# First norm of a hybrid decoder step: scale the rows of x before the transposes, and transpose raw x in a place of its own

## The chip, the cores and the metric

One core of a Trainium2 chip runs the whole kernel as one launch. The metric is the device time of one execution in microseconds (us), median of several runs. TensorE is called PE in the profile, VectorE DVE, ScalarE ACT, GpSimd POOL, and SyncE, whose queue starts the DMAs, SP.

## The reference, cut to what matters

One layer of a decoder trunk is computed for 512 prompt positions and for 8 samples of 8 positions, 576 tokens in all, with 1024 features. The part that matters here is the first norm and what uses x:

```python
def rmsnorm(x, w):
    xf = xf * lax.rsqrt(jnp.mean(xf * xf, axis=-1, keepdims=True) + EPS)
    return (xf * w.astype(F32)).astype(x.dtype)
...
    xn = rmsnorm(x, norm1_w)
    proj = xn @ w_in            # 1024 x 6928, feeds four token mixers
    gates = sigmoid(xn @ w_merge + b_merge)
    x = x + merged @ w_out      # raw x comes back here
    x = x + ConvFFN(rmsnorm(x, norm2_w))
```

(The last five lines are condensed from the reference.) So the token factor rsqrt(mean(x^2)) belongs to a row of x, the weight norm1_w to a column, and the raw x is wanted again only much later, for the residual sum.

## The kernel before, in words

All big products are done on PE in three passes (high x high, high x low, low x high), so each operand is split into a rounded part `hi` and a remainder `lo`. The activations stand transposed: `K.xh[k]` and `K.xl[k]`, k = 0..7, hold 128 features by 576 tokens each (columns 0 to 511 prompt, 512 to 575 samples).

`front` makes them. It loads x in five tiles `xt` (tokens on partitions; four of 128 prompt tokens, one of 64 sample tokens), sums the squares per token (`ss`: ACT for tiles 0, 2, 4, DVE for 1 and 3), takes Sqrt on ACT and a reciprocal on DVE, and turns the factors on PE into a tile `rb` in which every partition holds the factors of all 576 tokens. Apart from that, PE transposes raw x (32 transposes of 128x128 for the prompt, 8 of 64x128 for the samples); ACT copies the result to `xT0..7` and `xTs`. DVE multiplies `xT` by norm1_w and `rb` into `xn` (line 387), ACT rounds `xn` to `xh`, and DVE (for k = 2 and 5 POOL) subtracts for `xl` (line 170, in `split`). The sample columns go the same way in one tile `xns` on POOL. All of that has the highest priority, 3 * HIGH.

`front` returns `vectors`, which `dense_stream` calls after the first projection, "u". Before the change it finishes the loads of small vectors (three transposes into the banks `dn`, copied by DVE at line 140) and stores `xTt` and `xTs` to DRAM (lines 396 and 397); the tail reads them for the residual.

`dense_stream` is the long chain of products: "u" (4 panels of w_in, each 2 column halves x 24 matmuls of 128x288), then "rw", "hg" and so on. Each half uses one PSUM bank of the pool `dn`, which has two banks; ACT evacuates it. Two streams of mixers run beside it with priority HIGH. The raw weights are loaded three panels ahead (`wraw`, 3 buffers) and split by ACT (`whi`) and DVE or POOL (`wlo`).

The program order on each engine is laid out when the kernel is built: a scheduler takes instructions by priority along a simulated timeline, and gives out buffers of a pool as they come free there. On the chip each engine then runs its list strictly in that order. So an edit at one place can lay later instructions out in another order too.

Of the kernel before, what the change touches and what calls it, by code (L numbers as in the profile page):

```python
# [8 lines left out]
F32 = mybir.dt.float32  # L9
F32R = mybir.dt.float32r  # L10
AF = mybir.ActivationFunctionType
ALU = mybir.AluOpType
# [3 lines left out]
P = 128  # L16
D = 1024
TP = 512
NS = 8
LS = 8  # L20
T = TP + NS * LS
# [3 lines left out]
EPS = 1e-6  # L25
# [15 lines left out]
class Kern:  # L41
# [49 lines left out]
    def turn(self, out, x):  # L91

        sl = slice(x.base_partition(), x.base_partition() + x.shape[0])
        self.nc.tensor.transpose(out, x, self.ident[sl, sl])  # L94
# [230 lines left out]
def front(K):  # L325

    nc, tc, I = K.nc, K.tc, K.I
    K.columns()
    K.xh = [K.xnp.tile([P, T], F32R, name=f"xh{k}") for k in range(8)]
    K.xl = [K.xnp.tile([P, T], F32R, name=f"xl{k}") for k in range(8)]  # L330
    xTd = K.dram.tile([8, P, T], F32, name="xTd")
    K.xT = [xTd[k] for k in range(8)]
    xp, xs = I["x_prompt"][0], I["x_sample"].rearrange("b t d -> (b t) d")
    fp = K.fp
    with tc.high_priority(offset=3 * HIGH):
        pre = fp.tile([P, 1], F32, name="pre")
        nc.scalar.activation(pre, K.eps, AF.Sqrt)
        xt = []
        for i in range(5):
            r = P if i < 4 else T - 4 * P  # L340
            t = fp.tile([P, D], F32, name=f"xt{i}")
            nc.sync.dma_start(out=t[:r, :], in_=xp[i * P:(i + 1) * P, :] if i < 4 else xs)
            xt.append((t, r))
            if i == 0:
                K.load_group(0, fp)()

        ss = fp.tile([P, 5], F32, name="ssq")
        nc.vector.memset(ss, 1.0)
        for i, (t, r) in enumerate(xt):
            q = fp.tile([P, D], F32, tag=f"xq{i % 2}", bufs=1, name=K.n("xq"))  # L350
            if i % 2:
                nc.vector.tensor_tensor(out=q, in0=t, in1=t, op=ALU.mult)
                nc.vector.tensor_reduce(out=ss[:, i:i + 1], in_=q, op=ALU.add, axis=mybir.AxisListType.X)
            else:
                nc.scalar.activation(q[:r, :], t[:r, :], AF.Square, accum_out=ss[:r, i:i + 1])
        nc.scalar.activation(ss, ss, AF.Sqrt, bias=K.eps, scale=1.0 / D)
        nc.vector.reciprocal(out=ss, in_=ss)
        rb = fp.tile([P, T], F32, name="rb")
        pb = K.ps(of="b")
        for i, (t, r) in enumerate(xt):  # L360
            if i == 4:
                nc.vector.tensor_copy(out=rb[:, :TP], in_=pb)
                pb = K.ps(of="b")
            o = i * P if i < 4 else 0
            K.turn(pb[:, o:o + r], ss[:r, i:i + 1].to_broadcast([r, P]))
        nc.vector.tensor_copy(out=rb[:, TP:], in_=pb[:, :T - TP])

        t, r = xt[4]
        ps = K.ps(of="b")
        for k in range(8):  # L370
            K.turn(ps[:, k * r:(k + 1) * r], t[:r, k * P:(k + 1) * P])
        pv = ps.rearrange("p (k t) -> p k t", k=8)
        xTs = fp.tile([P, 8, r], F32, name="xTs")
        nc.scalar.copy(out=xTs, in_=pv)
        xns = fp.tile([P, 8, r], F32, name="xns")
        nc.gpsimd.tensor_tensor(out=xns, in0=xTs, in1=K.vcs("norm1_w", 0, 8).unsqueeze(2).to_broadcast([P, 8, r]), op=ALU.mult)
        nc.gpsimd.tensor_tensor(out=xns, in0=xns, in1=rb[:, TP:].unsqueeze(1).to_broadcast([P, 8, r]), op=ALU.mult)
        xTt = []
        for k in range(8):
            ps = K.ps(of=("a", "a0", "a2", "a0")[k % 4])  # L380
            for i in range(4):
                K.turn(ps[:, i * P:(i + 1) * P], xt[i][0][:, k * P:(k + 1) * P])
            xT = fp.tile([P, TP], F32, name=f"xT{k}")
            nc.scalar.copy(out=xT, in_=ps)
            xTt.append(xT)
            xn = fp.tile([P, TP], F32, tag="xn", bufs=3, name=K.n("xn"))
            nc.vector.scalar_tensor_tensor(out=xn, in0=xT, scalar=K.vc("norm1_w", k), in1=rb[:, :TP], op0=ALU.mult, op1=ALU.mult)
            K.split(K.xh[k][:, :TP], K.xl[k][:, :TP], xn, nc.gpsimd if k in (2, 5) else nc.vector)
            K.split(K.xh[k][:, TP:], K.xl[k][:, TP:], xns[:, k], nc.gpsimd)
    rest = [K.load_group(i, fp) for i in range(1, len(K.vgroups))]  # L390

    def vectors():
        for turn in rest:
            turn()
        for k in range(8):
            nc.sync.dma_start(out=K.xT[k][:, :TP], in_=xTt[k])
        nc.sync.dma_start(out=xTd[:, :, TP:].rearrange("k p t -> p k t"), in_=xTs)
        K.halve("rw_w0", "rw_a0", "b_merge", "ssd_conv_b", "s5_glu_b", "ssd_conv_w")
    return vectors

# [1906 lines left out]
@with_exitstack  # L2307
def hybrid_step(ctx, tc, I, O):
    K = Kern(ctx, tc, I, O)
    e = ctx.enter_context  # L2310
    K.xnp = e(tc.tile_pool(name="xn", bufs=1))
    K.stage = e(tc.tile_pool(name="stage", bufs=2))
    K.wraw = e(tc.tile_pool(name="wraw", bufs=3))
    K.wsp = e(tc.tile_pool(name="wsp", bufs=5))
    K.fc = ExitStack()
    K.fp = K.fc.enter_context(tc.tile_pool(name="front", bufs=1))
    K.vectors = front(K)
    drive(K, [(mix_stream(K, "a", ("rw",)), "a"), (mix_stream(K, "b", ("s5", "hg", "ssd")), "b"), (dense_stream(K), None)])
    K.spare = {"t": ["c"]}
    K.banks(4, c=2, w=2)  # L2320
    K.stream = "t"
    tail(K)
    K.pst.close()
# [26 lines left out]
```

## Time and profile before

| what | value |
|---|---|
| median of 3 runs | 1688.13 us |
| lowest, highest run | 1680.99, 1700.95 us |
| the profiled execution, its own time | 1685.1 us |
| its span, first to last instruction | 1683.4 us |
| PE busy | 1591.3 us (95%) |
| DVE, ACT, POOL busy | 70%, 41%, 47% |
| mean granted PE clock | 0.965 of full |

The busy shares are means over the whole span; the first 65 us, where the change lies, look different from the rest. The lowest and the highest run of the same kernel stand 1.2% apart.

### The profile page before, as it was taken

How to read it: one execution, taken by the hardware profiler on the slowest of the kernel's cores; microseconds unless marked ns; L12 is line 12 of the kernel's file. 1: busy time of each engine (PE TensorE's matmuls, PEld its weight loads, DVE VectorE, ACT ScalarE, POOL GpSimd, SP SyncE). 2: the span in 40 equal slices, each digit the busy share in tenths (PEclk: the TensorE clock that was granted, in tenths of full speed). 3: DMA queues.
4: the chain of work that ended last, by engine and by line, in shares of the span. 5: the costliest groups of instructions: out<-in, count | busy, mean ns of one | idle time of the engine just before them, and what ended most of it. 6: DMA issues, size and time to landing. Idle time of an engine off the chain costs nothing. (4 is left out here: it accounts for less than half of the span.)

```text
span 1683.4 us, 33091 instructions
## 1 busy us (share of the span) xinstructions
PE 1591.3 (95%) x12344; PEld 1445.8 (86%) x12344; DVE 1179.6 (70%) x2566; ACT 691.8 (41%) x1489; POOL 785.4 (47%) x1013
## 2 busy tenths in 40 slices
PE   5998999999999999999999999998999999999997
PEld 4987888888788888878888888998998999899997
DVE  7888886988684398343367553685489966975985
ACT  6333232333433345233244443432456634643653
POOL 5545342444522454232354542375667734744750
PEclk7999897899999999899999999999999999999999
DMA  7545452544472365343265543764323232232232
GB/s 202 136 122 152 130 140 59 159 136 113 134 202 73 101 165 173 87 104 93 87 178 148 169 133 106 233 199 142 112 84 89 80 109 63 88 89 82 82 108 72
DMA packets 356453, 207.64 MB, mean 123 GB/s; under 512 B 110884, under 2 KB 328357, under 8 KB 356293
## 3 DMA queue, kind: packets, MB, share of 16 engines
q1 hardware_dynamic: 356293, 205.53, 43.6%
q8 instruction: 97, 1.59, 0.4%
q14 instruction: 63, 0.52, 0.1%
HBM read 151.54 MB, written 53.02 MB: 122 GB/s over the span
## 5 line engine op out<-in xcount | busy, mean ns | idle before, releaser
L224 PE MATMUL dn<-xl,whi 128*128 128x288 f32 x1392 | 425.6, 306 | 2.0 <-DVE xl L170 1.6
L223 PE MATMUL dn<-xh,whi 128*128 128x288 f32 x1392 | 424.9, 306 | 2.4 <-ACT gst L432 0.9
L225 PE MATMUL dn<-xh,wlo 128*128 128x288 f32 x1392 | 424.9, 305 | 0.0
L225 PEld LDWEIGHTS dn<-xh,wlo 128*128 128x128 f32 x1392 | 267.6, 192 | 14.6 <-issue 11.2
L223 PEld LDWEIGHTS dn<-xh,whi 128*128 128x128 f32 x1392 | 267.5, 192 | 14.3 <-issue 7.3
L224 PEld LDWEIGHTS dn<-xl,whi 128*128 128x128 f32 x1392 | 267.6, 192 | 12.8 <-issue 6.2
L169 ACT CAST whi<-wraw 128x512 fp32r<-128x512 f32 (+1 forms) x278 | 173.5, 628 | 234.8 <-PE dn L224 227.3
L170 POOL TENSOR_TENSOR wlo<-wraw,whi 128x512 fp32r<-128x512 f32 x92 | 127.4, 1385 | 170.6 <-ACT whi L169 162.7
L170 DVE TENSOR_TENSOR wlo<-wraw,whi 128x512 fp32r<-128x512 f32 (+1 forms) x186 | 156.1, 841 | 66.4 <-ACT whi L169 58.0
L262 PE MATMUL dn<-big,whi 128*128 128x288 f32 x528 | 108.6, 298 | 8.7 <-DVE raw L679 2.9
L247 POOL TENSOR_TENSOR wlo<-wraw,whi 128x512 fp32r<-128x512 f32 x66 | 90.1, 1372 | 48.1 <-ACT whi L246 48.0
L262 PE MATMUL dn<-xh,whi 128*128 128x288 f32 x352 | 104.8, 299 | 4.7 <-ACT whi L246 4.0
L223 PE MATMUL dn<-yh,whi 128*128 128x288 f32 x352 | 103.9, 299 | 4.5 <-DVE g L489 3.3
L262 PE MATMUL dn<-xh,wlo 128*128 128x288 f32 x352 | 103.6, 298 | 4.4 <-POOL wlo L247 4.4
L224 PE MATMUL dn<-yl,whi 128*128 128x288 f32 x352 | 104.6, 298 | 2.1 <-DVE yl L167 2.1
L225 PE MATMUL dn<-yh,wlo 128*128 128x288 f32 x352 | 104.7, 299 | 0.0
L262 PE MATMUL dn<-xl,whi 128*128 128x288 f32 x352 | 103.5, 295 | 0.0
L223 PE MATMUL dn<-ah,whi 128*128 128x288 f32 (+2 forms) x324 | 95.1, 298 | 1.5 <-ACT ah L169 1.5
L224 PE MATMUL dn<-al,whi 128*128 128x288 f32 (+2 forms) x324 | 95.5, 296 | 0.6 <-DVE al L170 0.6
L262 PEld LDWEIGHTS dn<-big,whi 128*128 128x128 f32 x528 | 84.3, 188 | 12.4 <-ACT su L286 4.5
L225 PE MATMUL dn<-ah,wlo 128*128 128x288 f32 (+2 forms) x324 | 95.0, 295 | 0.0
L262 PE MATMUL dn<-big,wlo 128*128 128x288 f32 x264 | 77.7, 295 | 0.1
(749 smaller groups left out, 4105.6 us busy)
## 6 DMA issues: line engine op xcount, KB each, us to landing
wraw<-w_in SPq DMA_DIRECT2D x55, 512.0 KB
wraw<-ffn_up SPq DMA_DIRECT2D x44, 512.0 KB
wraw<-w_merge SPq DMA_DIRECT2D x32, 512.0 KB
gate<-gst SPq DMA_DIRECT2D x32, 288.0 KB
g<-gate SPq DMA_DIRECT2D x32, 288.0 KB
wraw<-ffn_down SPq DMA_DIRECT2D x16, 448.0 KB
pd_hg<-st SPq DMA_DIRECT2D x16, 288.0 KB
wraw<-w_br_ssd SPq DMA_DIRECT2D x8, 512.0 KB
```

The costliest lines, as they stand in the source:

```text
L169: nc.scalar.copy(out=hi, in_=src)
L170: lo_engine.tensor_tensor(out=lo, in0=src, in1=hi.bitcast(F32), op=ALU.subtract)
L223: nc.tensor.matmul(ps, wh, xh[k][:, sl], start=k == 0, stop=False)
L224: nc.tensor.matmul(ps, wh, xl[k][:, sl], start=False, stop=False)
L225: nc.tensor.matmul(ps, wl, xh[k][:, sl], start=False, stop=k == len(wt) - 1)
L247: TT[eng](out=lo, in0=src, in1=hi.bitcast(F32), op=ALU.subtract)
L262: nc.tensor.matmul(ps, wt[:, k], x, start=start and k == 0 and i == 0, stop=k == n - 1 and i == 2, skip_group_check=not start)
```

## The change

The sum of squares of tile 3 moves from DVE to ACT, and the factor is computed by DVE alone, with eight small operations on a 128x5 tile (`K.rsqrt`: one bit trick and two Newton steps), so the Sqrt on ACT and its early table load go. There is no `rb` any more: each row tile of x is multiplied by its factors into `xr` (tiles 0 and 2 on ACT, 1 and 3 on DVE, 4 on POOL). PE transposes `xr`. The split then reads the PSUM bank directly, with norm1_w as its scale: ACT writes `xh` and DVE `xl` for all eight k. The sample columns follow after the eight prompt groups. Raw x is transposed a second time inside `vectors`, after "u": for each k four prompt transposes into one bank `dn`, one sample transpose into another, two copies by ACT into a tile `xT` (2 buffers), and one store of 288 KB.

```diff
--- before.py
+++ after.py
@@ -333,8 +333,6 @@
     xp, xs = I["x_prompt"][0], I["x_sample"].rearrange("b t d -> (b t) d")
     fp = K.fp
     with tc.high_priority(offset=3 * HIGH):
-        pre = fp.tile([P, 1], F32, name="pre")
-        nc.scalar.activation(pre, K.eps, AF.Sqrt)
         xt = []
         for i in range(5):
             r = P if i < 4 else T - 4 * P
@@ -346,55 +344,54 @@
 
         ss = fp.tile([P, 5], F32, name="ssq")
         nc.vector.memset(ss, 1.0)
+        xr = [fp.tile([P, D], F32, name=f"xr{i}") for i in range(5)]
         for i, (t, r) in enumerate(xt):
-            q = fp.tile([P, D], F32, tag=f"xq{i % 2}", bufs=1, name=K.n("xq"))
-            if i % 2:
-                nc.vector.tensor_tensor(out=q, in0=t, in1=t, op=ALU.mult)
-                nc.vector.tensor_reduce(out=ss[:, i:i + 1], in_=q, op=ALU.add, axis=mybir.AxisListType.X)
+            if i == 1:
+                nc.vector.tensor_tensor(out=xr[i], in0=t, in1=t, op=ALU.mult)
+                nc.vector.tensor_reduce(out=ss[:, i:i + 1], in_=xr[i], op=ALU.add, axis=mybir.AxisListType.X)
             else:
-                nc.scalar.activation(q[:r, :], t[:r, :], AF.Square, accum_out=ss[:r, i:i + 1])
-        nc.scalar.activation(ss, ss, AF.Sqrt, bias=K.eps, scale=1.0 / D)
-        nc.vector.reciprocal(out=ss, in_=ss)
-        rb = fp.tile([P, T], F32, name="rb")
-        pb = K.ps(of="b")
+                nc.scalar.activation(xr[i][:r, :], t[:r, :], AF.Square, accum_out=ss[:r, i:i + 1])
+        nc.vector.tensor_scalar(out=ss, in0=ss, scalar1=1.0 / D, scalar2=EPS, op0=ALU.mult, op1=ALU.add)
+        rs, y1, y2 = (fp.tile([P, 5], F32, name=f"rsq{i}") for i in range(3))
+        K.rsqrt(rs, ss, y1, y2)
+
         for i, (t, r) in enumerate(xt):
-            if i == 4:
-                nc.vector.tensor_copy(out=rb[:, :TP], in_=pb)
-                pb = K.ps(of="b")
-            o = i * P if i < 4 else 0
-            K.turn(pb[:, o:o + r], ss[:r, i:i + 1].to_broadcast([r, P]))
-        nc.vector.tensor_copy(out=rb[:, TP:], in_=pb[:, :T - TP])
-
-        t, r = xt[4]
-        ps = K.ps(of="b")
-        for k in range(8):
-            K.turn(ps[:, k * r:(k + 1) * r], t[:r, k * P:(k + 1) * P])
-        pv = ps.rearrange("p (k t) -> p k t", k=8)
-        xTs = fp.tile([P, 8, r], F32, name="xTs")
-        nc.scalar.copy(out=xTs, in_=pv)
-        xns = fp.tile([P, 8, r], F32, name="xns")
-        nc.gpsimd.tensor_tensor(out=xns, in0=xTs, in1=K.vcs("norm1_w", 0, 8).unsqueeze(2).to_broadcast([P, 8, r]), op=ALU.mult)
-        nc.gpsimd.tensor_tensor(out=xns, in0=xns, in1=rb[:, TP:].unsqueeze(1).to_broadcast([P, 8, r]), op=ALU.mult)
-        xTt = []
+            f = rs[:r, i:i + 1]
+            if i in (0, 2):
+                nc.scalar.activation(xr[i][:r, :], t[:r, :], AF.Copy, scale=f)
+            else:
+                (nc.gpsimd if i == 4 else nc.vector).tensor_scalar(out=xr[i][:r, :], in0=t[:r, :], scalar1=f, scalar2=None, op0=ALU.mult)
         for k in range(8):
             ps = K.ps(of=("a", "a0", "a2", "a0")[k % 4])
             for i in range(4):
-                K.turn(ps[:, i * P:(i + 1) * P], xt[i][0][:, k * P:(k + 1) * P])
-            xT = fp.tile([P, TP], F32, name=f"xT{k}")
-            nc.scalar.copy(out=xT, in_=ps)
-            xTt.append(xT)
-            xn = fp.tile([P, TP], F32, tag="xn", bufs=3, name=K.n("xn"))
-            nc.vector.scalar_tensor_tensor(out=xn, in0=xT, scalar=K.vc("norm1_w", k), in1=rb[:, :TP], op0=ALU.mult, op1=ALU.mult)
-            K.split(K.xh[k][:, :TP], K.xl[k][:, :TP], xn, nc.gpsimd if k in (2, 5) else nc.vector)
+                K.turn(ps[:, i * P:(i + 1) * P], xr[i][:, k * P:(k + 1) * P])
+            K.split(K.xh[k][:, :TP], K.xl[k][:, :TP], ps, None, K.vc("norm1_w", k))
+
+        r = T - TP
+        ps = K.ps(of="b")
+        for k in range(8):
+            K.turn(ps[:, k * r:(k + 1) * r], xr[4][:r, k * P:(k + 1) * P])
+        xns = fp.tile([P, 8, r], F32, name="xns")
+        nc.vector.tensor_tensor(out=xns, in0=ps.rearrange("p (k t) -> p k t", k=8),
+                                in1=K.vcs("norm1_w", 0, 8).unsqueeze(2).to_broadcast([P, 8, r]), op=ALU.mult)
+        for k in range(8):
             K.split(K.xh[k][:, TP:], K.xl[k][:, TP:], xns[:, k], nc.gpsimd)
     rest = [K.load_group(i, fp) for i in range(1, len(K.vgroups))]
 
     def vectors():
         for turn in rest:
             turn()
+
         for k in range(8):
-            nc.sync.dma_start(out=K.xT[k][:, :TP], in_=xTt[k])
-        nc.sync.dma_start(out=xTd[:, :, TP:].rearrange("k p t -> p k t"), in_=xTs)
+            xT = fp.tile([P, T], F32, tag="xT", bufs=2, name=K.n("xT"))
+            for lo, hi in ((0, 4), (4, 5)):
+                ps = K.psdense()
+                n = (hi - lo) * P if lo == 0 else T - TP
+                for i in range(lo, hi):
+                    t, r = xt[i]
+                    K.turn(ps[:, (i - lo) * P:(i - lo) * P + r], t[:r, k * P:(k + 1) * P])
+                nc.scalar.copy(out=xT[:, lo * P:lo * P + n], in_=ps[:, :n])
+            nc.sync.dma_start(out=K.xT[k], in_=xT)
         K.halve("rw_w0", "rw_a0", "b_merge", "ssd_conv_b", "s5_glu_b", "ssd_conv_w")
     return vectors
 
```

`K.rsqrt`, `K.split`, `K.turn` and `K.psdense` are unchanged. `split` with a scale is the form that the second half of the kernel used already:

```python
        if scale is not None:
            nc.scalar.activation(hi, src, AF.Copy, scale=scale)
            nc.vector.scalar_tensor_tensor(out=lo, in0=src, scalar=scale, in1=hi.bitcast(F32), op0=ALU.mult, op1=ALU.subtract)
            return
```

## Rows read from the trace of the kernel before

**Rows 1.** The page, parts 1 and 2: busy time, and the clock in 40 slices.

```profile
PE 1591.3 (95%) x12344; PEld 1445.8 (86%) x12344; DVE 1179.6 (70%) x2566; ACT 691.8 (41%) x1489; POOL 785.4 (47%) x1013
...
PEclk7999897899999999899999999999999999999999
```

**Rows 2.** Windows: each engine's busy time, then PE clock, DMA share, GB/s.

```profile
24.00:37.00 13.00, 8.32 (x29) 6.21 (x29) 13.00 (x23) 7.49 (x27) 10.01 (x10) 0.50 0.69 217
37.00:61.00 24.00, 23.69 (x177) 23.23 (x176) 22.21 (x108) 11.12 (x22) 9.71 (x23) 1.00 0.64 161
61.00:64.40 3.40, 0.70 (x6) 0.24 (x4) 3.26 (x15) 0.92 (x2) 2.69 (x8) 0.99 0.40 66
200.00:1250.00 1050.00, 1018.52 (x8180) 899.04 (x8180) 666.38 (x1405) 388.42 (x862) 457.56 (x552) 0.96 0.47 134
```

**Rows 3.** Timeline, 12 to 24 us: start, length, engine, line, operation.

```profile
14.53 0.19 ACT L355 ACTIVATION_READ_ACCUMULATOR xq<-xt 64x1 f32 x1
...
15.56 2.06 ACT L169 CAST whi<-wraw 128x512 fp32r<-128x512 f32 x2
...
17.93 0.32 ACT L356 ACTIVATE ssq<-ssq,epsc 128x5 f32<-128x5 f32 x1
...
18.96 0.85 PE L94 MATMUL mx<-ident,ssq 128*128 128x128 f32 x5 [2.02 <-DVE ssq L357]
...
22.21 3.14 DVE L387 SCALAR_TENSOR_TENSOR xn<-xT,vecs,rb 128x512 f32<-128x512 f32 x3
...
23.81 0.61 PE L223 MATMUL dn<-xh,whi 128*128 128x288 f32 x1 [0.46 <-ACT xh L169]
```

**Rows 4.** Timelines of DVE and POOL, 37 to 40 us: the last pieces of xl.

```profile
37.67 0.68 DVE L170 TENSOR_TENSOR xl<-xn,xh 128x512 fp32r<-128x512 f32 x1
...
37.68 1.98 POOL L170 TENSOR_TENSOR xl<-xns,xh 128x64 fp32r<-128x64 f32 x5
```

**Rows 5.** Groups by line and shape, 0 to 45 us: count, busy us, mean ns.

```profile
L387 DVE SCALAR_TENSOR_TENSOR xn<-xT,vecs,rb 128x512 f32<-128x512 f32 x8 | 6.9, 889 | 0.0
...
L170 DVE TENSOR_TENSOR xl<-xn,xh 128x512 fp32r<-128x512 f32 x6 | 5.0, 834 | 0.0
...
L384 ACT COPY xT<-mx 128x512 f32<-128x512 f32 x8 | 4.5, 602 | 1.4 <-PE mx L94 1.4
...
L1048 DVE TENSOR_SCALAR exk<-exk 128x16 f32<-128x16 f32 x4 | 0.7, 168 | 0.1
```

**Rows 6.** Line 94, transposes of x, 12 to 13 us and 16.5 to 17 us: ns min/median/max.

```profile
L94 PE MATMUL mx<-ident,xt x4: 421/421/476, 12.1 to 12.8; 128*128 128x128 f32 x4
L94 PEld LDWEIGHTS mx<-ident,xt x4: 183/228/231, 12.1 to 12.6; 128*128 128x128 f32 x4
...
L94 PE MATMUL mx<-ident,xt x4: 273/314/421, 16.1 to 16.7; 128*128 128x128 f32 x4
L94 PEld LDWEIGHTS mx<-ident,xt x2: 140/178/217, 16.4 to 16.6; 128*128 128x128 f32 x2
```

**Rows 7.** Timeline, 61 to 70 us: the end of "u" and the vectors stage.

```profile
61.01 0.27 PE L94 MATMUL dn<-ident,vraw 128*128 128x128 f32 x1
...
63.33 0.40 PE L94 MATMUL dn<-ident,vraw 128*128 128x128 f32 x2 [2.05 <-DVE vecs L140]
...
64.38 0.61 PE L223 MATMUL dn<-xh,whi 128*128 128x288 f32 x1 [0.66 <-DVE vecs L140]
...
69.40 0.40 ACT L414 COPY st<-dn 128x288 f32<-128x288 f32 x1 [7.41 <-DMA wup<-rw_a_up]
```

**Rows 8.** Timeline of SP's queue, 73 to 83 us: stores and reloads of a 288 KB panel.

```profile
73.81 0.53 SPq L422 DMA_DIRECT2D pd_rw<-st  x1
79.43 0.33 SPq L1465 DMA_DIRECT2D raw<-pd_rw  x1
79.88 0.36 SPq L422 DMA_DIRECT2D pd_rw<-st  x1
...
82.50 0.46 SPq L1465 DMA_DIRECT2D raw<-pd_rw  x1
```

**Rows 9.** PE's waits, 90 to 200 us: total us, times, longest.

```profile
PE mxrw L1571 <- DVE tB L1565: 5.3, 2, 4.7
```

**Rows 10.** Line 1165, a DVE copy of 256 elements: ns min/median/max.

```profile
L1165 DVE COPY s5br<-s5u x1: 281/281/281, 57.2 to 57.2; 128x256 f32<-128x256 f32 x1
```

## The prediction, as it was put on record

> **What bounds the kernel now.** I read the page first, then windows by stage, then the timeline of the first 70 us, then waits. PE is busy for 95% of the span [rows 1], and between 200 and 1250 us it works 1018.5 of 1050 us while no other engine passes 64% [rows 2]: from there on the kernel is PE's own pace, and a microsecond that the dense products lose or win early is still there at the end. The change lies ahead of that, in two places with other limits. From 24 to 37 us DVE is busy for all of 13.0 us, and PE, at half clock, makes only 29 instructions where it makes 177 in the next 24 us [rows 2]: there the products wait for the pieces of xh and xl. From 61.0 to 64.4 us, after "u", PE works 0.7 us of 3.4 [rows 2]: it waits 2.05 and 0.66 us for DVE to empty the banks of the small vectors, while ACT stands idle for 7.41 us [rows 7].
>
> At 37 to 61 us a product takes 24/177 = 0.136 us. "u" has 192 of them, 26 us; it ends at 61.0, so it ends as if it had run at full pace from 35.0. What the front wins is how far that point moves forward.
>
> **The front, part by part.** *Head.* The last sum of squares is there at 14.72, but Sqrt runs on ACT only at 17.93, behind two rounding casts of weights (15.56, 2.06 us); then come the reciprocal, PE's turn at 18.96, the copies to `rb`, and the first `xn` at 22.21; the first product starts at 23.81 [rows 3]. After: eight dependent DVE operations on 128x5. A DVE operation on 128x16 takes 0.168 us [rows 5], so 1.3 us, taken as 1.6 with the handovers (an estimate): factors at 16.3. The casts still fill ACT until 17.6. Then `xr` 0 and 2 on ACT: twice the elements of an `xT` copy (0.602 us [rows 5]), so 1.2 us each at most, until 20.0. `xr` 1 and 3 on DVE: four times the copy of 256 elements in 0.281 us [rows 10], 1.1 us each at most, done before. `xr` 4 on POOL is needed last. The last transpose of the first group and ACT's `xh` (0.6 us) give 20.9 for the first product: 2.9 us earlier.
>
> *Body.* From 22.21 to the last prompt `xl`, 38.35 [rows 3, 4], are 16.1 us of DVE: 6.9 for eight `xn`, 5.0 for six `xl` [rows 5], so 4.2 for other work (weight splits, the S5 tables). After, the eight `xn` are gone, but all eight `xl` are DVE's, in the two-operand form that line 387 has now, and from PSUM. The nearest rows are 0.834 and 0.889 us [rows 5]; with 0.85 that is 6.8, plus one `xns` of 0.85 and the same 4.2: 11.9 us from 20.9, so 32.8, 5.6 us earlier. ACT loses eight `xT` copies (4.5 us) and gains two `xr` (2.4) and one square; its eight `xh` stay. PE now has the transposes on the path: 0.23 us apart at half clock [rows 6], 0.92 for a group of four, about the same pace as DVE's 0.85. *Sample columns.* POOL takes 1.98/5 = 0.40 us for each of eight small `xl`, 3.2 us, and ends at 39.66 now [rows 4]; after, with `xns` made near 31.5, at about 35, 4.7 us earlier, and the products of the second half are wanted only then. POOL also loses two large `xl` and two multiplications.
>
> I take 5.5 us for the front, between the two. Its bounds: 2.9, if only the head is won, and 8, if some 2.5 us of DVE's other work slips behind the front.
>
> The stores of xT leave SP's queue near 31 us. I cost that at nothing: the weights of "u" were split by then or are loaded three panels ahead. Without this cover it would be a gain. The early Sqrt and its table load ran before x had landed: nothing too.
>
> **Raw x, the price.** Eight groups now stand between "u" and "rw". For a group PE fills one bank `dn` with four transposes, ACT empties it, and the next group wants that bank again, because the other holds the sample columns. So PE and ACT take turns. The transposes: 3 x 0.14 + 0.27 = 0.7 us at full clock, 3 x 0.23 + 0.42 = 1.1 at half [rows 6]; the copy 0.6 [rows 5]; two handovers of 0.1 (an estimate). That is 1.5 to 1.9 us for a group, 12.0 to 15.4 for eight; PE's busy share of some half leaves the clock open, so I take 1.75, 14 us. ACT has the room (7.41 us idle, eight copies of 0.6 and eight of the sample's, smaller). Behind the waiting transposes stand on PE the first products of "rw", which want the same two banks; behind the copies on ACT the next weight casts; on SP, behind stores that wait for ACT, the loads for RWKV and the next panel of w_in. The panels for "rw" already landed cover that.
>
> What hides some of it: the 2.7 us in which PE waits for DVE at this very place [rows 7]. Two banks serve both, so I count 1 us (0 to 2.7). Later, between 90 and 200 us, PE waits 5.3 us in a mixer for DVE [rows 9]; if the mixer's DVE work is not late as well, part of the delay ends there. But that mixer is fed by "rw", which is late; I count 1.5 (0 to 5.3).
>
> The clock, first as the rows show it: transposes of 421 ns at 12.1 to 12.8 us become 273 ns at 16.7, when PE had run nothing but transposes for four microseconds [rows 6]; so here a stretch of transposes alone brought the full clock. The Trainium skill (TensorE: Matmul & The Clock Gate, Part 4: PE-mode transpose) says that transposes do not engage the full clock; the trace disagrees. By that rule all groups would run at half clock, 15.4 us in place of 14, and the front's groups at 0.92 in place of 0.85, 0.6 later. It would make the change 2.0 us worse, the fourth case below.
>
> **Sum.** -5.5 + 14 - 1 - 1.5 = +6.0 us. The profiled execution, 1685.1, becomes 1691; it stands 3.0 under the median of the runs, 1688.13, which becomes 1694. A difference under 1% (17 us) is about what a measurement of this kernel can't tell from no change: its three runs lie 1.2% apart.
>
> **Rivals.** *Hidden.* All terms at their good ends: -8 + 12 - 2.7 - 5.3 = -4, 1684. For it: ACT and DVE's waits leave room just there; against it: one bank per group is a strict turn, and PE is the pace later. *Stores, the slow side.* `xT` has two buffers, so the copy of group k+2 waits until the store of k has landed. Two stores of the same size show bounds: issued 79.88, read back from 82.50 on, at most 2.6 us; issued 73.81, read back at 79.43, at most 5.6 [rows 8]. With a copy and a sample copy of 0.8, a group takes half of (landing + 0.8): 1.7 us at 2.6, hidden beneath the banks; 3.2 at 5.6, 25.6 us for eight: -5.5 + 25.6 - 2.5 = +17.6, 1706. From a landing of about 2.7 us on it sets the pace; from 5.4 on the loss passes 1%. *It doesn't speed the front.* If DVE, with all `xl` from PSUM, keeps the pace of now, only the head's 2.9 is left: -2.9 + 14 - 2.5 = +8.6, 1697. *Clock rule.* By the case above +8.0, 1696; the row speaks against it. *Laid out anew.* Everything behind is ordered by a simulated timeline, so stages far from the change can shift. The mean clock of 0.965 means 3.5% of 1683 us, 59 us, lost to half clock, in slices all along [rows 1]; a quarter of that either way is 15 us: 1679 or 1709 around the forecast. Nothing in the profile says which way.
>
> **Chances.** Forecast, with its terms between the ends, 0.40; hidden 0.20; stores 0.12; front not faster 0.08; clock rule 0.04; anew, better 0.08, worse 0.08. The range of 8 in 10 goes from 1677 to 1708: it leaves out about half of each outer case and the spread of a median of such runs. Faster by over 1% (under 1671): 0.07, the better half of "anew" and the tail of "hidden". Slower by over 1% (over 1705): 0.16, most of "stores" and "anew, worse". The rest, 0.77, lies within.
>
> **What the profile after would show.** If the steps are right: no `xn` group, eight `xl` of some 0.85 us on DVE from PSUM, the first product near 21 us, "u" ending near 55.5 in place of 61.0; then eight groups at `dn`, transposes of xt alternating with ACT copies, 1.5 to 1.9 us each, and the first product of "rw" near 71 in place of 64.4. Stores as the limit would show as ACT's copies waiting for a DMA. What would make it wrong: raw transposes that run inside "u" or between products, in gaps that cost nothing; groups paced by stores; a front that still waits, for the clock or for casts on ACT ahead of `xr`; or PE's half-clock stretches after 100 us moving by more than both terms.

## The result, and the profile after

| kernel | median us | lowest to highest | runs | ratio to before, 95% interval |
|---|---|---|---|---|
| before | 1683.94 | 1677.81 to 1700.95 | 22 | |
| after | 1697.47 | 1689.5 to 1712.43 | 22 | 1.0083 (1.0063 to 1.0103) |

The change makes the kernel 0.8% slower: 13.5 us by the medians, 11 to 17 by the interval. The median lies 3.5 us over the forecast of 1694, inside the range of 1677 to 1708 and inside "within 1%". In part that is luck. The difference was forecast as +6 and came out twice as large; and the three runs of before that the forecast stood on had a median of 1688.13, where these 22 have 1683.94, from which the sum gives 1690. So the sum has to be gone through. The profiled execution of after took 1691.0 us (span 1689.3), the very figure of the sum; that is luck too, for it is the third lowest of its 22 runs, while that of before stood 1.2 us over the median of its kernel. A single pair of traces differs here by 5.9 us where the medians differ by 13.5.

The page of after, parts 1 and 2, against [rows 1]:

```profile
PE 1589.9 (94%) x12379; PEld 1446.4 (86%) x12379; DVE 1163.9 (69%) x2566; ACT 699.2 (41%) x1498; POOL 784.9 (46%) x1010
...
PEclk9788887999999999999999999999999999999999
```

PE is still the bound; span less busy time, it was idle for 99.4 us in place of 92.1. In the clock line the first slice of 42 us rose from 0.7 to 0.9 of the full clock, the second fell from 0.9 to 0.7: the new front won clock, and the raw-x stage lost it. But the line flatters the start. The profile records no clock ahead of the first rise, at 16.5 us in before and 25.4 in after, and the line counts that time as full; the transposes below show that it was half. The windows of the same stretches, against [rows 2] (busy time of PE, PEld, DVE, ACT, POOL, then PE clock, DMA share, GB/s):

```profile
24.00:37.00 13.00, 12.99 (x99) 12.22 (x98) 11.63 (x35) 9.22 (x27) 5.23 (x13) 1.00 0.49 134
...
54.20:77.80 23.60, 18.57 (x102) 13.94 (x100) 21.15 (x83) 8.39 (x22) 7.19 (x19) 0.64 0.43 121
...
20.00:24.00 4.00, 3.68 (x17) 3.45 (x17) 3.84 (x5) 3.56 (x6) 4.00 (x3) 1.00 0.47 97
...
59.50:76.60 17.10, 16.22 (x87) 12.64 (x88) 15.05 (x52) 5.97 (x17) 2.96 (x5) 0.50 0.40 126
```

From 24 to 37 us PE makes 99 instructions, from 25.4 on at full clock; it made 29 at half. "u" ends at 54.2 in place of 60.9, and what stood between it and the first product of "rw" has grown from 3.4 us to 23.6, at 0.64 of the clock: PE is at half from 59.5 to 76.6.

The head of the front, timeline of after, against [rows 3]:

```profile
13.44 0.17 DVE L354 TENSOR_SCALAR ssq<-ssq 128x5 f32<-128x5 f32 x1 [4.54 <-ACT xr L353]
...
14.46 0.21 DVE L1082 COPY s5ldb<-s5ld 16x128 f32<-16x128 f32 x1 [0.85 <-DMA s5ld<-s_log_dt]
14.61 0.15 DVE L176 TENSOR_SCALAR rsq<-ssq 128x5 int32<-128x5 int32 x1
...
15.07 1.08 DVE L170 TENSOR_TENSOR wlo<-wraw,whi 128x512 fp32r<-128x512 f32 x1
...
16.14 1.08 DVE L170 TENSOR_TENSOR wlo<-wraw,whi 128x512 fp32r<-128x512 f32 x1
16.84 1.77 POOL L170 TENSOR_TENSOR wlo<-wraw,whi 128x512 fp32r<-128x512 f32 x1 [13.80 <-ACT whi L169]
17.13 1.49 DVE L178 TENSOR_TENSOR rsq<-rsq 128x5 f32<-128x5 f32 x1
...
18.86 0.17 DVE L180 SCALAR_TENSOR_TENSOR rsq<-rsq,rsq 128x5 f32<-128x5 f32 x1
...
19.12 2.19 ACT L361 ACTIVATE xr<-xt,rsq 128x1024 f32<-128x1024 f32 x2 [1.43 <-DVE rsq L180]
...
19.94 2.29 DVE L363 TENSOR_SCALAR xr<-xt,rsq 128x1024 f32<-128x1024 f32 x2
...
20.32 3.71 PE L94 MATMUL mx<-ident,xr 128*128 128x128 f32 x16 [15.69 <-ACT xr L361]
...
23.69 0.59 PE L223 MATMUL dn<-xh,whi 128*128 128x288 f32 x1
...
25.45 0.66 PE L94 MATMUL mx<-ident,xr 128*128 128x128 f32 x4
```

The eight small operations are cheap, but other work stands between them on DVE: a copy that waits for its DMA, two weight splits of 1.08 us, and one step of 1.49 us in place of 0.17. The factors are there at 19.03, not 16.3. DVE's two `xr`, which I had done before ACT's, follow one more weight split and end at 22.23. A table load on ACT remains, 1.28 us at 4.32, ahead of the first square; ACT waits for x behind it, so it cost nothing here.

The 16 transposes from 20.32 on take 3.71 us, 0.22 us apart: the pace that [rows 6] gave for the half clock (0.23). The four at 25.45 take 0.66 us, 0.13 apart. So PE was at half until 25.4 us, though the column of the windows shows 1.00 for 20 to 24.

The pieces of `xl`, one group per line (duration ns min/median/max, first and last start), against [rows 4, 5]:

```profile
L167 DVE SCALAR_TENSOR_TENSOR xl<-mx,vecs,xh x8: 741/748/751, 23.5 to 30.3; 128x512 fp32r<-128x512 f32 x8
L170 POOL TENSOR_TENSOR xl<-xns,xh x8: 319/324/336, 27.9 to 29.9; 128x64 fp32r<-128x64 f32 x8
```

There is no `xn` left, and the last prompt `xl` ends at 30.3 + 0.75 = 31.0 in place of 38.35. PE's timeline between "u" and "rw", against [rows 7]:

```profile
57.16 0.40 PE L94 MATMUL dn<-ident,vraw 128*128 128x128 f32 x2 [2.59 <-DVE vecs L140]
58.22 0.86 PE L94 MATMUL dn<-ident,xt 128*128 128x128 f32 x5 [0.66 <-DVE vecs L140]
59.55 1.41 PE L94 MATMUL dn<-ident,xt 128*128 128x128 f32 x5 [0.47 <-ACT xT L393]
61.34 1.41 PE L94 MATMUL dn<-ident,xt 128*128 128x128 f32 x5 [0.38 <-ACT xT L393]
62.69 0.69 PE L94 MATMUL mxs<-ident,W 128*128 128x128 f32 x2
63.40 1.41 PE L94 MATMUL dn<-ident,xt 128*128 128x128 f32 x5
...
66.57 1.54 PE L94 MATMUL mxs<-ident,W 128*128 128x128 f32 x6
67.91 1.35 PE L94 MATMUL dn<-ident,xt 128*128 128x128 f32 x5
69.19 0.63 PE L1240 MATMUL mxs<-s5cbr,W 128*128 128x32 f32 x2
...
72.74 1.23 PE L1264 MATMUL mxs<-U,Mz 128*64 128x72 f32 x16
73.90 1.41 PE L94 MATMUL dn<-ident,xt 128*128 128x128 f32 x5
75.25 1.23 PE L1264 MATMUL mxs<-U,Mz 128*64 128x72 f32 x16
76.40 0.92 PE L94 MATMUL dn<-ident,xt 128*128 128x128 f32 x5
77.84 0.40 PE L223 MATMUL dn<-xh,whi 128*128 128x288 f32 x1 [0.52 <-ACT xT L393]
```

The turns of PE and ACT at one bank are there, [0.38 <-ACT xT], a group every 1.8 to 2.1 us; the first group ran at full clock (0.86 for five transposes) and most of the last (0.92), those between took 1.35 to 1.41 at half. Between the groups, and ahead of the last two, PE runs S5 products (tile mxs). They had to be done anyway; before, they stood later.

SP's queue and the chain of waits of after:

```profile
59.64 10.45 SPq L394 DMA_DIRECT2D xTd<-xT  x6
73.47 5.77 SPq L1249 DMA_DIRECT2D Mt<-Kc  x7
79.34 1.07 SPq L394 DMA_DIRECT2D xTd<-xT  x2
82.78 0.34 SPq L528 DMA_DIRECT2D csi<-state_rwkv_shift  x1
```

```profile
79.34 0.60 SPq L394
...
80.04 2.59 DMA xTd<-xT
...
82.82 0.27 POOL rwm L1369 x2
```

The last stores stand behind seven loads of `Mt`. When the last has landed, POOL starts the tables of the RWKV mixer (`rwm`), DVE starts `rwoka` (82.8 in place of 64.25), and SP the mixer's loads: this memory belonged to the front until then. I had not foreseen that wait.

### The profile page after: what moved, and what is told of

Read it like the earlier page. It is cut to its first block, busy times and chain, and to the rows that moved or that the text cites. A ratio compares the mean times of both kernels' runs of the same rounds, so it can differ in the third digit from the quotient of the medians.

```text
span 1689.3 us, 33181 instructions
## 1 busy us (share of the span) xinstructions
PE 1589.9 (94%) x12379; PEld 1446.4 (86%) x12379; DVE 1163.9 (69%) x2566; ACT 699.2 (41%) x1498; POOL 784.9 (46%) x1010
## 4 chain that ended last, share of the span: by engine, by line
PE 57%; DVE 20%; DMA 8%; issue 6%; POOL 4%; ACT 3%; SPq 2%; POOLq 0%; DVEq 0%; ACTq 0%
PE dn L224 11%; PE dn L223 11%; PE dn L225 11%; PE dn L262 6%; DVE mx L546 2%; DVE accs L553 2%; DVE wlo L170 2%; DVE wlo L247 1%; PE mxssd L2072 1%; PE mxs L1318 1%; PE mxhg L899 1%; DVE mx L253 1%; PE mx L94 1%; DMA s_rwkv<-tB 1%; DVE wc L253 1%
## 5 line engine op out<-in xcount | busy, mean ns | idle before, releaser
L170 DVE TENSOR_TENSOR wlo<-wraw,whi 128x512 fp32r<-128x512 f32 (+1 forms) x186 | 151.1, 813 | 64.5 <-ACT whi L169 55.8
```

Of the source, the lines that this page charges most:

```text
L170: lo_engine.tensor_tensor(out=lo, in0=src, in1=hi.bitcast(F32), op=ALU.subtract)
```

## The experiments

Each run also lists its mean granted clock. Over 65 runs of the kernel before, the runs with a clock higher by 0.01 were 9.8 us shorter (straight line, correlation -0.84); over the 22 of after 10.0 us (-0.89). So the table has a column of estimates: the mean span of a kernel's runs, moved by 10 us per 0.01 to a clock of 0.966. Two cautions go with it. The slope is a correlation among runs of one kernel; that it holds from one kernel to another was not shown. And the mean clock counts the time ahead of the first record as full: 14.7 to 17.8 us in before, its two other layouts, late_raw_old_front and the two raw_early, 24.7 to 30.5 in the other eight. Counted as half, these eight would stand some 0.003 to 0.004 lower against the rest, 3 to 4 us in the estimate.

| kernel | ratio (95% interval) | mean clock | span at 0.966, estimate |
|---|---|---|---|
| before | 1 | 0.9676 | 1684 |
| before_n5 | 0.9975 (0.9946 to 1.0003) | 0.9671 | 1680 |
| before_n7 | 1.0028 (1.0002 to 1.0054) | 0.9641 | 1686 |
| after | 1.0083 (1.0063 to 1.0103) | 0.9653 | 1696 |
| after_n7 | 1.0062 (1.0032 to 1.0092) | 0.9664 | 1692 |
| after_n8 | 1.0108 (1.0077 to 1.0138) | 0.9615 | 1697 |
| act_stores | 1.0071 (1.0043 to 1.0099) | 0.9655 | 1694 |
| stage_first | 1.0103 (1.0059 to 1.0146) | 0.9617 | 1695 |
| late_raw_old_front | 1.0067 (1.0043 to 1.0091) | 0.9647 | 1691 |
| no_raw | 0.9916 (0.9885 to 0.9948) | 0.9747 | 1678 |
| no_raw_n7 | 0.9953 (0.9927 to 0.9979) | 0.9752 | 1684 |
| raw_early | 1.0090 (1.0056 to 1.0124) | 0.9667 | 1698 |
| raw_early_n7 | 1.0113 (1.0077 to 1.0150) | 0.9648 | 1701 |
| mixer_banks | 1.0107 (1.0069 to 1.0145) | 0.9632 | 1698 |

**The front without raw x.** no_raw stores rows of x as they are; the stage is gone.

```diff
-                    K.turn(ps[:, (i - lo) * P:(i - lo) * P + r], t[:r, k * P:(k + 1) * P])
...
-            nc.sync.dma_start(out=K.xT[k], in_=xT)
+            nc.sync.dma_start(out=K.xT[k][:, :TP], in_=xt[k % 4][0][:, (k // 4) * TP:(k // 4 + 1) * TP])
```

> The changed kernel without any transposing of raw x: the rows of x are stored untransposed in the place of xT, so the residual is not the reference's; the stores have the bytes of the kernel before. The front alone. If the stage after "u" is the loss: "rw" starts near 58 us, 6 to 7 us earlier than in the kernel before, and the time is 5 to 7 us under it (1677 to 1679). If the front gain is lost behind: 1684. If the new order behind is the loss: above 1690.

Measured: 1671.8 us, 0.9916. The first product of "rw" came at 59.2 (64.4 before), and PE's clock in the first 90 us stands at 0.98 (0.89 before; both count the start as full):

```profile
0.00:90.00 90.00, 65.65 (x479) 63.52 (x480) 66.62 (x239) 42.85 (x87) 48.71 (x140) 0.98 0.67 177
```

So the new front wins, and the transposes of raw x lose more than it wins. That the gain at the end (14 us by the ratio, 11 by the medians) is larger than the 5.2 us at this place asked for a second layout, below.

**The stage without the front.** late_raw_old_front keeps the old front and adds the stage behind "u".

```diff
-            nc.sync.dma_start(out=K.xT[k][:, :TP], in_=xTt[k])
...
+                    K.turn(ps[:, (i - lo) * P:(i - lo) * P + r], t[:r, k * P:(k + 1) * P])
+                nc.scalar.copy(out=xT[:, lo * P:lo * P + n], in_=ps[:, :n])
+            nc.sync.dma_start(out=K.xT[k], in_=xT)
```

> The front of the kernel before, with its raw transposes and xT copies, and after "u" raw x is transposed once more as in the changed kernel, with its stores in place of the early ones. It has the price without the gain. If the stage after "u" is the loss: "rw" starts some 17 to 20 us later than in the kernel before, and the time is 15 to 20 us over it (1699 to 1704), more than the changed kernel. If the price is swallowed later by waits of PE: under 1690. If the scaled front itself makes the changed kernel slower: no change from before (1684).

Measured: 1693.95 us, 1.0067, less than the 1699 to 1704 of the expectation. "rw" began at 85.5, 21.2 us late, after a stage like that of the change (windows):

```profile
61.00:85.50 24.50, 19.59 (x110) 14.96 (x108) 17.42 (x62) 8.73 (x23) 8.09 (x19) 0.65 0.46 132
```

The mixer's `rwoka` came at 91.9, the latest of all kernels, and yet this one lost no more than the change did (the intervals overlap). So with the stage behind "u" the new front won nothing at the end, where without it it did: the two have no fixed prices that add up.

**The stage off the path.** raw_early puts the raw transposes ahead of the scaled ones, where PE is idle, in the mixers' banks, and stores them where before did.

```diff
         K.rsqrt(rs, ss, y1, y2)
+        for k in range(8):
+            ps = K.ps(of=("a", "a0", "a2", "a0")[k % 4])
+            for i in range(4):
+                K.turn(ps[:, i * P:(i + 1) * P], xt[i][0][:, k * P:(k + 1) * P])
...
-            nc.sync.dma_start(out=K.xT[k], in_=xT)
+            nc.sync.dma_start(out=K.xT[k][:, :TP], in_=xTt[k])
```

> The scaled front as in the changed kernel, but raw x is transposed ahead of the scaled rows, on the PE that stands idle there, into the mixers' banks, and stored as in the kernel before; no raw x after "u". If the turns of PE and ACT after "u" are the loss (20 us between the end of "u" and the first product of "rw", against 3.5): "u" still ends some 5 to 7 us earlier than before, "rw" starts near 59 us, and the time is about 5 us under the kernel before (some 1679). If the front's 7 us are worth nothing at the end: no change from before (1684). If the loss comes from the new order of everything behind: above 1690, whatever the front does.

Measured: 1700.41 us, 1.009. "rw" began 4.2 us earlier than before, and the kernel is still as slow as the change. My theory then, that the loss is the stage's place behind "u", falls. Windows of raw_early show what the other place does to PE:

```profile
12.00:16.00 4.00, 3.94 (x24) 3.58 (x24) 1.45 (x9) 4.00 (x9) 0.00 (x0) 1.00 1.19 276
16.00:20.00 4.00, 0.43 (x4) 0.44 (x5) 3.96 (x5) 4.00 (x6) 3.81 (x2) 0.81 1.02 129
20.00:24.00 4.00, 2.61 (x16) 2.24 (x14) 3.96 (x5) 4.00 (x6) 4.00 (x4) 0.50 0.32 74
24.00:28.00 4.00, 3.90 (x19) 3.33 (x18) 3.73 (x14) 3.95 (x16) 3.45 (x10) 0.50 0.62 167
```

PE works from 12 to 16 us, all but rests until 19.6 while it waits for `xr`, and is at half clock from 18.5 to 28.7. Its first rise came at 15.1 us, after nothing but transposes, 421 ns for one of 128x128 until then (timings behind it, ns min/median/max):

```profile
L94 PE MATMUL mx<-ident,xt x8: 272/273/421, 14.7 to 15.7; 128*128 128x128 f32 x8
```

The early transposes do not keep the clock down for longer, though. It is back at full at 28.0 and 28.7 us in the two raw_early kernels, at 24.7 to 30.5 in the eight others with the new front, and at 37.0 to 40.3 in the four with the old one. Nor is the front where raw_early loses: "u" ended at 56.3 (no_raw 55.2), in the second layout, below, at 56.8 (57.4). It loses later (windows of before, then of raw_early):

```profile
90.00:330.00 240.00, 224.73 (x1849) 198.72 (x1848) 200.52 (x641) 75.28 (x189) 100.28 (x167) 0.87 0.49 124
```

```profile
90.00:330.00 240.00, 217.69 (x1804) 193.38 (x1805) 197.70 (x633) 75.75 (x190) 104.20 (x170) 0.90 0.50 129
```

PE is idle for 22.3 us there (21.1 in the second layout), in the three layouts of before for 15.3, 14.8 and 17.7. The mixer's first `shd` on POOL (timelines, no_raw, then raw_early) comes 6.3 us later than in no_raw, although "rw" began only 1.1 us later, and PE waits 4.0 us for what follows it, ACT's `rwwa`. But before, which does not lose, has it at 84.61.

```profile
78.94 0.72 POOL L1459 TENSOR_TENSOR shd<-raw 128x320 f32<-128x320 f32 x1
```

```profile
85.26 0.72 POOL L1474 TENSOR_TENSOR shd<-raw 128x320 f32<-128x320 f32 x1
```

**Other banks for the stage.** mixer_banks lets the stage use banks of the mixers in place of `dn`.

```diff
-                ps = K.psdense()
+                ps = K.ps(of=("a", "a0", "a2", "a0")[k % 4] if lo == 0 else "b")
```

> The changed kernel, but the raw transposes after "u" use the mixers' banks (four for the prompt, two for the samples) in place of the two that the products need; work and stores are the same. If the strict turns on the two banks are the loss: the products of "rw" no longer stand behind them, PE pays only its 40 transposes (5.6 us at 0.14), and the time falls by some 10 to 14 us to 1684 to 1688. If the loss is that the RWKV mixer's memory is free only when the last store of raw x has landed (82.7 us in the changed kernel): it falls only as far as that store moves forward; with the store still near 80 us the time stays above 1692.

Measured: 1703.26 us, 1.0107. "rw" began at 63.5, 0.9 us earlier than before, with no turns at `dn`; the kernel did not gain. The raw transposes now ran inside "u" from 32.3 us on, and "u" ended at 59.1 in place of 54.2; the mixer's memory was free at 69.7. So neither the turns nor the late "rw" nor the late release is the loss as a whole.

**How much of it is the order behind.** Unused DVE copies in `vectors` lay nearly everything behind them out anew: one of 128x64 (before_n5), three of 128x64 (both n7), two of 128x128 (after_n8).

```diff
         for turn in rest:
             turn()
+        with tc.high_priority(offset=HIGH):
+            for i in range(3):
+                nudge = fp.tile([P, 64], F32, name=f"nudge{i}")
+                nc.vector.tensor_copy(out=nudge, in_=K.vecs[:, :64])
```

> The kernel before with one more DVE copy of 128x64 (some 0.2 us, its result unused) among the small vectors, at the mixers' priority. Its own work can't be seen in the time. The scheduler lays out nearly everything behind it anew: on DVE 1540 of 2568 instructions keep their order relative to each other. If the layout of what lies behind matters little: no change from before (within 4 us of 1683). If the loss of the changed kernel is within what a new layout does by itself: more than 5 us away from before, to either side.

> The same with three such copies (some 0.6 us): another layout, on DVE 1760 of 2568 instructions in the old order. If the layout matters little: within 4 us of before. If it does: more than 5 us away, and not by the same amount as with one copy.

> The changed kernel with the same three copies: another layout of the changed kernel, on DVE 1698 of 2568 instructions in its order. If the stage after "u" and the late release of the front's memory make the loss of 14 us: again 1.0 to 1.2% over the kernel before, less only by noise. If most of the loss is the layout that this change happened to get: several us away from it, to either side.

> The changed kernel with two such copies of 128x128 (some 0.6 us), a third layout of the changed kernel (2054 of 2568 on DVE in its order). As the run before: within 4 us of the changed kernel if its own stages make the loss, several us away if the layout does.

Measured: 0.9975 and 1.0028 for before, 1.0062 and 1.0108 for after. A layout is worth some 0.25% (4 us) either way, and the slowest of before lies under the fastest of after, if not by more than their intervals. The means of the three layouts are 1.0001 and 1.0084: the loss belongs to the change, not to its layout.

**The two front kernels in a second layout.** The same three copies.

> The changed kernel without the transposes of raw x (rows of x are stored untransposed, so the later residual sums use wrong data), and with three unused DVE copies of 128x64 that lay the rest out anew (1775 of DVE's 2568 instructions in the old order). no_raw stood at 0.9916. If its gain was the front's alone, 5 to 7 us as its first product of rw showed (-5.2), this one is at 0.995 to 0.998. If leaving out the transposes is worth the whole 14 us whatever the layout, it is at 0.991 to 0.993. Near 1.000 the first would have been a lucky layout altogether.

> The new front with the raw transposes ahead of the scaled ones, and three unused DVE copies of 128x64 that lay the rest out anew (1822 of DVE's 2568 instructions in the old order). raw_early stood at 1.009 though its first product of rw came 4.2 us sooner than before. If the order behind was bad luck, this one is at 0.996 to 1.001, better than the changed kernel by the stage behind u; if something of the new front costs later whatever the layout, it is at 1.006 to 1.011 again.

Measured: 0.9953 and 1.0113. Without raw x the kernel is faster in both layouts, by 0.5 to 0.8%; with raw x ahead of the front it is slower in both, by 0.9 to 1.1%. raw_early was no bad luck. In the clock column the two kernels without raw x stand alone: 0.975, where all twelve others lie between 0.9615 and 0.9676.

**The late release.** act_stores issues the eight stores from ACT, so that they don't wait behind `Mt`; stage_first gives the stage a higher priority. Both leave the order behind nearly as it is.

```diff
-            nc.sync.dma_start(out=K.xT[k], in_=xT)
+            nc.scalar.dma_start(out=K.xT[k], in_=xT)
```

```diff
+        with tc.high_priority(offset=2 * HIGH):
             for k in range(8):
```

> The changed kernel with its eight stores of xT issued by ACT instead of SP; the order of the other work stays nearly as it is (2561 of DVE's 2568 instructions stand in the old order), so this is a local test. In the changed kernel the last two stores stood on SP behind seven loads of Mt and were issued at 79.34, and the mixer's tables were free at 82.8. Release theory (the mixer's late tables are what the stage costs): the stores leave right after their copies, near 77 to 78, the tables are written some 2 us sooner, and the time falls by 1 to 2 us against the changed kernel, ratio to the kernel before 1.007. Theory of the turns alone (only PE's and ACT's alternation at the banks costs): no change, 1.008. Both fall if ACT, now issuing DMAs between its copies, spaces the groups further: then over 1.010.

> The changed kernel with the raw-x stage at a higher priority, order of the rest nearly unchanged (2560 of DVE's 2568 instructions in the old order). In the changed kernel groups seven and eight stood on PE behind the S5 products (73.90 and 76.40 instead of some 69.7 and 71.5). Release theory: with eight groups in one run the last store is issued near 74 and lands near 77, the tables of the mixer come 5 to 6 us sooner, and the time falls by 4 to 6 us, ratio to the kernel before 1.005. Theory of the turns alone: the S5 products, which filled the gaps between groups, only change places with them, and the time stays, 1.008.

Measured: 1695.47 us, 1.0071, and 1701.01 us, 1.0103. act_stores is where the release theory wanted it, but its interval holds 1.0083 too, and its stage also ran partly at full clock (16.1 us from the first raw group to "rw" in place of 19.6): PE's timeline has

```profile
71.18 0.41 PE L1240 MATMUL mxs<-s5cbr,W 128*128 128x32 f32 x2
...
73.73 0.86 PE L94 MATMUL dn<-ident,xt 128*128 128x128 f32 x5
```

where after has 0.63 and 1.41 us. In after PE has no gap from 65.2 us on and is at half until 76.6; in act_stores it has none from 67.3 on and is at full from 71.0. Why was not found. stage_first missed its aim: the last two groups still stand behind the S5 products on PE, and the last store left SP at 80.74, so it says nothing on the release. The price of the release stays open. It is not the main one: by the start of `rwoka`, 91.9 (late_raw_old_front), 86.9 (after_n7), 82.8 (after), 69.7 (mixer_banks) and 60.1 (raw_early) us, the ratios run 1.0067, 1.0062, 1.0083, 1.0107, 1.0090, without order.

No kernel with the reference's residual was faster than before beyond its interval.

## Why the prediction was right, and where its sum was not

**The front, -5.5: right at its place, by another way.** "u" ended 6.7 us earlier. The head, forecast at 2.9 of it, gave 0.1 (first product 23.69 for 23.81): I counted eight operations of 0.2 us and not what DVE's list puts between them, which made the factors 2.7 us late. The body gave the rest and more: from the first to the last, the eight `xl` took 7.5 us on DVE, not 11.9. One took 0.75 us, not 0.85, `xns` 0.68, and less than 1 us of other work or waiting stood between them, where I had kept 4.2: the case of my upper bound, DVE's other work slipping behind the front. And PE was at full clock from 25.4 us on. I had costed PE's half clock of [rows 2] as a given, but it goes with the old front, whose four kernels have the clock back at 37.0 to 40.3 us; the ten with the new one have it at 24.7 to 30.5.

**The stage, +14: the turns right in size, the delay larger.** From the end of "u" to "rw" it is 23.6 us. Before had 3.4 there and no_raw 4.0. So "rw" began at 77.84, 13.5 us late, where I had named 71. Of the 19.6 over no_raw, about 8.3 are S5 products at half clock (0.69 + 1.54 + 3.6 + 2 x 1.23), which before ran later; that leaves 11.3 for eight groups. Groups of 1.8 to 2.1 us at the half clock are what the working said for that end (1.9). The stores did not pace them: the one landing that the chain shows, 2.59 us, lies just under the 2.7 named as the point, and ACT's copies waited for PE, not for a store. That rival falls for this reason. The "front not faster" rival falls with the body.

The clock rule was a rival as well. The rows: the first raw group ran at full clock, the next ones and the S5 products among them at half, until 76.6; in act_stores two later groups ran at full again, after S5 products without a gap. The Trainium skill (TensorE: Matmul & The Clock Gate, Part 4: PE-mode transpose) has transposes not engage the full clock. The stage as a whole was nearer to that end than I forecast, 0.64; but in before [rows 6] and in raw_early the clock rose to full when PE had run nothing but such transposes, so the rule as stated does not hold here.

**The cover, -1, and later waits, -1.5: not collected.** PE still waited 2.59 and 0.66 us for DVE's vectors at [rows 7]'s place, ahead of the stage instead of ahead of "rw". The mixer's wait of [rows 9], for DVE's `tB`, did shrink, from 5.3 to 3.5 us, but the next one, for `tA`, grew from 1.6 to 3.2. The mixer was late together with "rw", through the release that I had not seen; that this is why no slack was left fits, but was not tested.

**The end.** The estimates at equal clock put the sum in order, to some 3 us (the spread between layouts) and with the cautions above. Before: 1683 (mean of three layouts). Without raw x: 1681 (two). After: 1695 (five kernels). On this path the front is worth about -2 in the end and the raw transposes behind "u" +14, 12 together, in place of the forecast's -5.5 and +11.5. On top stands the clock: 0.9663 before, 0.975 without raw x, 0.9641 after (means of the same kernels). At 10 us per 0.01 that is 9 us won by the new front and 11 lost by the raw transposes, 2 net; 12 + 2 is the measured 14. With the start counted as half, some 3 to 4 us of those 9 belong to the front itself. By the other path, the stage first, late_raw_old_front has 1691: +8 for the stage, and +4 for the front on top of it, from one layout. So the split is an estimate; what the runs show is that the kernel without the raw transposes is 0.5 to 0.8% faster than before, and with them behind "u" 0.6 to 1.1% slower. My case "laid out anew" had the clock as a toss of a coin. The layouts do toss it, by 0.003 or so; but leaving the raw transposes out raised it in both layouts, and that is no coin.

**What stays open.** Moved ahead of "u", where PE is idle, or into other banks and so into "u", the raw transposes cost as much as in the change: 1698, 1701 and 1698 at equal clock (raw_early, raw_early_n7, mixer_banks). Both layouts of raw_early show PE idle for some 3 to 7 us more than before between 90 and 330 us; why, and where the rest goes, was not found. Nor was the stage tried in memory of its own, which would have freed the mixer's tables.

## What to carry to other kernels

Read the clock of a kernel's start from the durations of equal instructions: the clock column showed 1.00 where transposes took 0.22 us each, and 0.13 a little later. Where a change has two parts, run each without the other: here the front gained without the raw transposes and gained nothing with them. When a stage is moved behind the point where a pool is given back, ask who waits for that memory, and read the chain of waits at the next user, not only at the stage. And where a scheduler lays the program out, time three layouts of both versions (a few unused copies do it) before a difference under 1% is put down to the edit.

## What was not expected of the hardware

A DVE step of 0.17 us took 1.49 us while POOL ran a split of two inputs from 16.84 to 18.61, and ended with it at 18.62. It is no single case; a little later in after (timeline):

```profile
32.49 0.17 DVE L1044 TENSOR_TENSOR exk<-exk,exr 128x16 f32<-128x16 f32 x1
32.59 1.62 POOL L170 TENSOR_TENSOR wlo<-wraw,whi 128x512 fp32r<-128x512 f32 x1 [2.40 <-ACT s5cr L1177]
32.70 1.54 DVE L1045 TENSOR_SCALAR exk<-exk 128x16 f32<-128x16 f32 x1
```

The DVE step ends at 34.24, POOL's at 34.21; the same step took 0.22 us at 34.48. The Trainium skill (SBUF — State Buffer, SBUF: two separate sides) says that DVE and POOL share a pair of ports as an exclusive lock, held for a whole instruction, and that the loser blocks; these rows agree with it. A chain of small DVE operations on the path can meet that at any step.

The mean clock of a whole execution differs from run to run of one kernel (0.952 to 0.973 over 22 runs of after), and most of the scatter of the times goes with it.
